# Decode attention: scores of the far old keys on VectorE, with key positions on partitions, and a far softmax of its own

## The chip, the cores and the metric

The kernel runs on one core of a Trainium2 chip. Its time is the device time of one execution in microseconds (us). TensorE (PE) multiplies matrices into PSUM, VectorE (DVE) and ScalarE (ACT) work elementwise and along rows, GpSimd (POOL) does small elementwise work, SyncE (SP) issues nearly all DMAs. Each engine runs its own instructions in the order of the program.

## What is computed

One decoder layer for 256 prompt tokens and 8 decode sequences of 8 new tokens (320 columns in all): a SwiGLU block, a token mixer, a second SwiGLU block. The mixer has an mLSTM branch and a branch of dilated attention with 8 heads of 128. The change is in the attention of the decode tokens. Cut to that:

```python
PATTERNS = ((128, 1), (512, 4), (2048, 16))          # window, dilation
for (w, d), bias in zip(PATTERNS, biases):
    idx = qi[:, None] - d * jnp.arange(w // d + 1)[None, :]
    s = jnp.einsum('bthe,btjhe->bhtj', q, k_all[:, idx]) + bias.T[None, :, None, :]
    m = jnp.max(s, axis=-1)
    p = jnp.exp(s - m[..., None])
    num, den = jnp.einsum('bhtj,btjhe->bthe', p, v_all[:, idx]), jnp.sum(p, axis=-1)
# the three (num, den, m) are joined by their maxima; 2048 old positions in the cache
```

Of the old positions the last 512 are near: all of them are multiplied, and a mask says how often each counts. The 96 far positions of a query (distance 528 to 2048 in steps of 16) are its own: query t of the 8 sees the positions 16 m + t, so the 8 queries of a sequence have 768 far positions between them and share none.

## The kernel before

All large weights are streamed: a chunk is 512 KB (four blocks of 128 rows by 256 columns). SP loads it (raw, 5 buffers), ScalarE casts it to hi, VectorE subtracts to get lo (3 buffers each, `split_upto`, L196 and L197), and TensorE runs 24 foreground matmuls (fg) with it. `run_job` (L242) goes through the chunks; with `split_upto(ci + HLB)` the chunk two ahead is split before chunk ci is multiplied. A chunk of casts can start when TensorE is done with the chunk whose buffer it takes.

All other work is written as Python generators that `run_job` steps between chunks: `every` at each chunk, `even` and `odd` at every second, `slow` at 8 of 15. `later(fn, n)` calls fn n chunks on; the DMAs are issued so. Background matmuls (bg, four PSUM tiles) stand in TensorE's program ahead of the chunk's own.

`sample_attention` (L586) is the only generator in `slow`. A unit u is a half of the heads (hg) and a sequence (b): 16 units, five steps each.
- Step 1: `pv(u - 1)` (probabilities times values), `scores(u)`, the scaled output (osb, L713), `soft(u)` (add of bias and mask, maximum, exponential).
- Step 2: `make_qbd(u + 1)` on GpSimd: the queries of the next unit, masked so that row 32 h + 8 i + t of the score tile is head h, group i of the keys, query t.
- Step 3: `probs(u)`: transposes of the probabilities, copies to SBUF, the sums. Steps 4 and 5 issue key loads only.

The old keys of a unit come in four tiles kd (a head each, 640 KB): four groups of 320 keys, 128 near ones and 192 far ones. The score tile thus has 128 rows (4 heads x 4 groups x 8 queries) and 328 columns: 128 near, 192 far (of which a row keeps every eighth, the mask drops the others), 8 new ones. Four matmuls in four column groups of TensorE (`tile_position`) make one step over 32 of the 128 rows of a head:

```python
for j in range(4):
    for h in range(4):
        mm(sp[32 * h:32 * h + 32, 0:320], qbd[:, 4 * h + j], KD[4 * u + h][:, j], j == 0, j == 3,
           tile_position=(0, 32 * h))
```

The values are multiplied in 11 steps of the same kind: 4 near, 6 far, 1 new. Every fourth unit `combine` (L735) transposes outputs and writes them to DRAM; after the last unit they are read back (ar) for the branch's projection w_pa.

## Time and profile before

| | |
|---|---|
| time, median of 3 | 2692.55 us (2691.93 to 2692.73) |
| the profiled execution | 2691.65 us |
| its span | 2689.9 us |
| mean granted TensorE clock | 0.998 |
| moved by DMA | 554.46 MB, 206 GB/s |

The profile is of one execution. "Busy" of PE is the time in which a matmul was under way; matmuls overlap, so the cost of a group is read from the starts. The chain that ended last goes back from the last instruction to what released it, step by step; an engine's share of it is what a change on this engine alone could move. A row of a group ends with its busy time, the mean ns of one, and the idle time of its engine ahead of it with what ended that. L numbers are lines of the kernel before.

### The profile page before, as it was taken

How to read it: one execution, taken by the hardware profiler on the slowest of the kernel's cores; microseconds unless marked ns; L12 is line 12 of the kernel's file. 1: busy time of each engine (PE TensorE's matmuls, PEld its weight loads, DVE VectorE, ACT ScalarE, POOL GpSimd, SP SyncE). 2: the span in 40 equal slices, each digit the busy share in tenths (PEclk: the TensorE clock that was granted, in tenths of full speed). 3: DMA queues.
4: the chain of work that ended last, by engine and by line, in shares of the span. 5: the costliest groups of instructions: out<-in, count | busy, mean ns of one | idle time of the engine just before them, and what ended most of it. 6: DMA issues, size and time to landing. Idle time of an engine off the chain costs nothing.

```text
span 2689.9 us, 49935 instructions
## 1 busy us (share of the span) xinstructions
PE 2674.8 (99%) x21176; PEld 2639.2 (98%) x21176; DVE 1430.7 (53%) x1706; ACT 1075.2 (40%) x1337; POOL 178.7 (7%) x222
## 2 busy tenths in 40 slices
PE   9999999999999999999999999999999999999998
PEld 9999999999999999999999999999999999999998
DVE  6544444444446554666655555655444454444445
ACT  5333333333335333455443444444333333333344
POOL 0100000000000000112211100000000000000000
PEclk9999999999999999999999999999999999999999
DMA  7554545445546678899999976655455454445443
GB/s 240 162 164 163 163 159 165 160 158 161 167 155 199 226 261 285 290 347 318 343 348 329 334 280 217 204 184 164 157 165 161 162 163 162 160 154 172 161 152 131
DMA packets 186684, 554.46 MB, mean 206 GB/s; under 512 B 26192, under 2 KB 53336, under 8 KB 186460
## 3 DMA queue, kind: packets, MB, share of 16 engines
q1 hardware_dynamic: 185740, 549.95, 60.5%
q8 instruction: 166, 2.72, 0.4%
q10 hardware_dynamic: 720, 1.31, 0.1%
q14 instruction: 58, 0.48, 0.1%
HBM read 519.98 MB, written 31.20 MB: 205 GB/s over the span
## 4 chain that ended last, share of the span: by engine, by line
PE 98%; DVE 1%; DMA 0%; ACT 0%; issue 0%; SPq 0%; DVEq 0%; ACTq 0%
PE fg L114 93%; PE bg L114 5%; PE bg L311 1%; DMA x<-in_x_t_dram 0%; DVE lo L197 0%; DVE x L1509 0%; DMA raw<-in_w_in_dram 0%; ACT hi L196 0%; DVE rows L781 0%; SPq L111 0%; ACT xh L1434 0%; DVE rows L790 0%; ACT lg L1497 0%; ACT hi L1424 0%; DVE x L1363 0%
## 5 line engine op out<-in xcount | busy, mean ns | idle before, releaser
L197 DVE TENSOR_TENSOR lo<-raw,hi 128x1024 fp32r<-128x1024 f32 (+1 forms) x780 | 958.1, 1235 | 919.4 <-ACT hi L196 895.9
L114 PE MATMUL fg<-xh,hi 128*128 128x320 f32 x4232 | 1271.4, 301 | 1.5 <-ACT hi L1424 1.5
L114 PE MATMUL fg<-xh,lo 128*128 128x320 f32 x4232 | 1261.6, 299 | 0.5 <-DVE lo L197 0.5
L114 PE MATMUL fg<-xl,hi 128*128 128x320 f32 x4232 | 1261.4, 299 | 0.0
L196 ACT CAST hi<-raw 128x1024 fp32r<-128x1024 f32 (+1 forms) x780 | 797.3, 1026 | 1039.6 <-PE fg L114 920.4
L114 PEld LDWEIGHTS fg<-xh,hi 128*128 128x128 f32 x4232 | 798.5, 189 | 8.9 <-issue 5.8
L114 PEld LDWEIGHTS fg<-xl,hi 128*128 128x128 f32 x4232 | 798.7, 189 | 0.8
L114 PEld LDWEIGHTS fg<-xh,lo 128*128 128x128 f32 x4232 | 798.6, 189 | 0.9 <-DVE lo L197 0.7
L114 PE MATMUL fg<-hh,hi 128*128 128x320 f32 x1408 | 421.3, 299 | 0.0
L114 PE MATMUL fg<-hl,hi 128*128 128x320 f32 x1408 | 421.0, 299 | 0.0
L114 PE MATMUL fg<-hh,lo 128*128 128x320 f32 x1408 | 421.0, 299 | 0.0
L114 PEld LDWEIGHTS fg<-hh,hi 128*128 128x128 f32 x1408 | 266.1, 189 | 0.1
L114 PEld LDWEIGHTS fg<-hl,hi 128*128 128x128 f32 x1408 | 266.1, 189 | 0.1
L114 PEld LDWEIGHTS fg<-hh,lo 128*128 128x128 f32 x1408 | 266.1, 189 | 0.0
L422 POOL TENSOR_TENSOR gt<-gt,rstd 128x640 f32<-128x640 f32 x44 | 68.2, 1549 | 1753.8 <-ACT gt L421 1753.8
L114 PE MATMUL fg<-bh,hi 128*128 128x320 f32 x512 | 153.3, 299 | 0.0
L114 PE MATMUL fg<-bl,hi 128*128 128x320 f32 x512 | 153.1, 299 | 0.0
L114 PE MATMUL fg<-bh,lo 128*128 128x320 f32 x512 | 153.1, 299 | 0.0
L114 PEld LDWEIGHTS fg<-bh,hi 128*128 128x128 f32 x512 | 96.8, 189 | 0.2 <-issue 0.2
L114 PEld LDWEIGHTS fg<-bl,hi 128*128 128x128 f32 x512 | 96.8, 189 | 0.0
L114 PEld LDWEIGHTS fg<-bh,lo 128*128 128x128 f32 x512 | 96.8, 189 | 0.0
L410 ACT CAST hh<-hf 128x640 fp32r<-128x640 f32 x44 | 34.7, 789 | 143.9 <-DVE hf L428 143.9
(266 smaller groups left out, 1217.6 us busy)
## 6 DMA issues: line engine op xcount, KB each, us to landing
raw<-in_w_in_dram SPq DMA_DIRECT2D x176, 512.0 KB
raw<-in_w_ffb_in_dram SPq DMA_DIRECT2D x176, 512.0 KB
raw<-in_w_ffa_in_dram SPq DMA_DIRECT2D x172, 512.0 KB
raw<-in_w_ffa_out_dram SPq DMA_DIRECT2D x80, 512.0 KB
kd<-in_old_k_dram SPq DMA_DIRECT2D x64, 640.0 KB
vt<-in_old_v_dram SPq DMA_DIRECT2D x80, 512.0 KB
raw<-in_w_ffb_out_dram SPq DMA_DIRECT2D x80, 512.0 KB
raw<-in_w_out_dram SPq DMA_DIRECT2D x32, 512.0 KB
```

The source lines that it names most:

```text
L114: T.matmul(out, a, b, start=start, stop=stop, **kw)
L196: S.copy(hi[:, :nk], t[:, :nk])
L197: V.tensor_tensor(lo[:, :nk], t[:, :nk], hi[:, :nk].bitcast(F32), op=OP.subtract)
L311: T.transpose(out, in_, ident[:k, :k])
L410: S.copy(h, xe)
L422: G.tensor_tensor(gt, gt, bcast(rstd, 2), op=OP.mult)
```

## The change

The keys are laid out anew on the host: near_k holds the near keys of two heads in a tile (nk, 512 KB, 32 of them), far_k the far keys with positions on partitions (fk, 128 positions x 2 groups x 512 columns of four heads, 512 KB, three a unit). Partition 16 t + i holds a position of query t. The score tile has 138 columns: 128 near, 8 new, one for the far maximum and one for the far sum.

- `aq_evac` transposes the decode queries to rows (two transposes for each pair of heads) and writes them to DRAM (qt_d). `load_qr` reads the 8 query rows of a unit back, each to 16 partitions (qr, 256 KB).
- `far_dots(u, n)`: VectorE multiplies a far tile by qr; the sums over the 128 columns of a head are a reduction on VectorE (n = 0 and 2) or eight activations with a sum on ScalarE (n = 1).
- `far_max`, `far_sum`: bias, the maximum over the 96 positions of a query by two 32x32 transposes, the exponential, the sum along the row. Four matmuls (fr by tsel) add the maximum and the sum over partitions and put them into columns 136 and 137 of the score tile.
- `soft` takes its maximum over near, new and far maximum; `probs` works out the two factors rw. `far_probs` spreads the far probabilities to the columns of their queries (pf), so that they need no transpose. `pv` makes near and far outputs apart, and VectorE adds the second to the first with its factor.
- The far work of unit u + 1 stands in the steps of unit u: dots 0 in step 1, dots 1 in step 2, dots 2 and the maximum in step 4, the sum in step 5. The loop over the units begins two steps later.
- In `numer` of the mLSTM an Abs on ScalarE takes the place of two VectorE instructions.

```diff
-SCOLS = 328
+SCOLS = 138
...
-            mk[:, i, t, 128 + t:320:8] = 0.0
             if i == 0:
-                mk[:, i, t, 320:328] = _logmult(t - np.arange(8))
+                mk[:, i, t, 128:136] = _logmult(t - np.arange(8))
+                mk[:, i, t, 136] = 0.0
+            mk[:, i, t, 137] = 0.0
...
+    tsel = (p[:, None] // 16 == q[None] % 8).astype(np.float32)
+    lead = (p[:, None] % 16 == 0).astype(np.float32)
+    c["mix"] = np.concatenate([bd, sel, sels, in4, qmask, cm, tsel, lead], axis=1)
...
-    RAWB, HLB, KDB = 5, 3, 6
+    RAWB, HLB, NKB, FKB = 5, 3, 3, 4
...
+        yield
+        yield
+        a = bg_tile()
+        for m in range(2):
+            tr(a[0:NS, m * 128:(m + 1) * 128], q[:, m, SEQ:NT])
+        s = m2_tile("qt")
+        S.copy(s[0:NS, 0:256], a[0:NS, 0:256])
+        later(lambda: dma(qt_d[:, p * 256:(p + 1) * 256], s[0:NS, 0:256]))
+        M["aq"] = p
...
+        def load_near(n):
+            if n < 32:
+                NK[n] = mxt([128, 2, 4, 128], "nk4", NKB, "nk")
+                dma(NK[n], I["near_k"][n].rearrange("p (h j c) -> p h j c", h=2, j=4))
+
+        def load_far(n):
+            if n < 48:
+                FK[n] = mxt([128, 2, 512], "fk", FKB, "fk")
+                dma(FK[n], I["far_k"][n].rearrange("p (a c) -> p a c", a=2))
+
+        def load_qr(u):
+            if u < 16:
+                hg, b = divmod(u, 8)
+                assert M["aq"] >= 2 * hg + 1
+                QR[u] = mxt([128, 512], "qr", 2, "qr")
+                dma(QR[u], raw_ap(qt_d[:], 8 * b * 1024 + hg * 512, [[1024, 8], [0, 16], [1, 512]]))
...
+        def far_dots(u, n):
+            if u > 15:
+                return
+            if n == 0:
+                SF[u] = mxt([128, 6, 4], "fs", 2, "fs")
+            t, sf = FK.pop(3 * u + n), SF[u]
+            V.tensor_tensor(t, t, bcast(QR[u], 2), op=OP.mult)
+            if n == 1:
+                for a in range(2):
+                    for h in range(4):
+                        x = t[:, a, h * 128:(h + 1) * 128]
+                        S.activation(x, x, AF.Copy, accum_out=sf[:, 2 + a, h:h + 1])
+            else:
+                V.tensor_reduce(sf[:, 2 * n:2 * n + 2].rearrange("p a h -> p (a h)"),
+                                t.rearrange("p a (h d) -> p (a h) d", h=4), op=OP.add, axis=AX.X)
+            later(lambda: load_far(3 * u + n + FKB), 1)
+
+        def far_max(u):
+            if u > 15:
+                return
+            sf = SF[u]
+            V.tensor_tensor(sf, sf, M["fb"][:, u // 8], op=OP.add)
+            V.tensor_reduce(fm[:, 0, 0:4], sf.rearrange("p c h -> p h c"), op=OP.max, axis=AX.X)
+            V.transpose(fm[:, 1], fm[:, 0])
+            V.tensor_reduce(fm[:, 2, 0:2], fm[:, 1].rearrange("p (s k) -> p s k", s=2), op=OP.max, axis=AX.X)
+            V.tensor_copy(fm[:, 1].rearrange("p (s k) -> p s k", s=2), bcast(fm[:, 2, 0:2], 16, 2))
+            V.transpose(fm[:, 2], fm[:, 1])
+            V.tensor_tensor(sf, sf, bcast(fm[:, 2, 0:4], 6), op=OP.subtract)
+            S.activation(sf, sf, AF.Exp)
+
+        def far_sum(u):
+            if u > 15:
+                return
+            V.tensor_scalar(fr[:, :, 0], fm[:, 2, 0:4], lead, None, op0=OP.mult)
+            V.tensor_reduce(fr[:, :, 1], SF[u].rearrange("p c h -> p h c"), op=OP.add, axis=AX.X)
+
+        def far_probs(u):
+            V.tensor_tensor(pf[:, 0:192].rearrange("p (a t) -> p a t", t=8),
+                            bcast(SF.pop(u).rearrange("p c h -> p (c h)"), 8, 2), bcast(tsel[:, 0:8], 24), op=OP.mult)
...
-        for _ in range(3):
-            yield
+        load_qr(0)
+        yield
+        load_qr(1)
+        yield
...
-                    mm(sp[32 * h:32 * h + 32, 0:320], qbd[:, 4 * h + j], KD[4 * u + h][:, j], j == 0, j == 3,
+                    mm(sp[32 * h:32 * h + 32, 0:128], qbd[:, 4 * h + j], NK[2 * u + h // 2][:, h % 2, j], j == 0, j == 3,
                        tile_position=(0, 32 * h))
             for h in range(4):
                 c = (4 * hg + h) * 64 + 8 * b
-                mm(sp[32 * h:32 * h + 32, 320:328], M["qS"][:, c:c + 32], M["kS"][:, c:c + 8],
+                mm(sp[32 * h:32 * h + 32, 128:136], M["qS"][:, c:c + 32], M["kS"][:, c:c + 8],
                    tile_position=(0, 32 * h))
+            for h in range(4):
+                mm(sp[32 * h:32 * h + 32, 136:138], tsel, fr[:, h], tile_position=(0, 32 * h))
...
-            V.tensor_reduce(sm[:, 0, 0:1], s, op=OP.max, axis=AX.X)
+            V.tensor_reduce(sm[:, 0, 0:1], s[:, 0:137], op=OP.max, axis=AX.X)
...
-            S.activation(s, s, AF.Exp, bias=sm[:, 3, 0:1], accum_out=sm[:, 4, 0:1])
+            S.activation(s[:, 0:136], s[:, 0:136], AF.Exp, bias=sm[:, 3, 0:1], accum_out=sm[:, 4, 0:1])
+            S.activation(s[:, 136:137], s[:, 136:137], AF.Exp, bias=sm[:, 3, 0:1])
...
-            cs = [(128, 0, 8 * i, i // 2, i % 2) for i in range(4)]
-            cs += [(128, 1, 8 * i, 2 + i // 2, i % 2) for i in range(4)]
-            cs += [(128, 2, 16 * i, 4, i) for i in range(2)]
-            cs += [(128, 3, 0, 5, None)]
-            for n, (k, slot, c, pc, half) in enumerate(cs):
-                v = VT[u, pc] if half is None else VT[u, pc][:, half]
+            cs = [(0, 8 * i, VT[u, i // 2][:, i % 2]) for i in range(4)] + [(1, 0, VT[u, 5])]
+            for n, (slot, c, v) in enumerate(cs):
                 for h in range(4):
-                    mm(ob[32 * h:32 * h + 32, 0:128], pts[0:k, slot, 32 * h + c:32 * h + c + 32],
-                       v[0:k, h * 128:(h + 1) * 128], n == 0, n == len(cs) - 1, tile_position=(0, 32 * h))
+                    mm(ob[32 * h:32 * h + 32, 0:128], pts[:, slot, 32 * h + c:32 * h + c + 32],
+                       v[:, h * 128:(h + 1) * 128], n == 0, n == 4, tile_position=(0, 32 * h))
+            for c in range(6):
+                v = VT[u, 2 + c // 2][:, c % 2]
+                for h in range(4):
+                    a = 8 * (4 * c + h)
+                    mm(ob[32 * h:32 * h + 32, 128:256], pf[:, a:a + 32],
+                       v[:, h * 128:(h + 1) * 128], c == 0, c == 5, tile_position=(0, 32 * h))
...
-            tr(pt[:, 128:256], s[:, 128:256])
-            tr(pt[0:72, 256:384], s[:, 256:328])
-            S.copy(pts[:, 0:2, 0:128], pt[:, 0:256].rearrange("p (c n) -> p c n", c=2))
-            V.tensor_copy(pts[0:64, 2, 0:128], pt[0:64, 256:384])
-            S.copy(pts[64:128, 2, 0:120], pt[0:64, 264:384])
-            V.tensor_copy(pts[0:8, 3, 0:128], pt[64:72, 256:384])
+            tr(pt[0:8, 128:256], s[:, 128:136])
+            S.copy(pts[:, 0, 0:128], pt[:, 0:128])
+            S.copy(pts[0:8, 1, 0:128], pt[0:8, 128:256])
             V.transpose(sm[:, 1], sm[:, 4])
             V.tensor_reduce(sm[:, 5, 0:8], sm[:, 1].rearrange("p (i t) -> p t i", i=4), op=OP.add, axis=AX.X)
-            V.reciprocal(sm[:, 5, 0:8], sm[:, 5, 0:8])
             V.transpose(sm[:, 6], sm[:, 5])
-
+            V.scalar_tensor_tensor(rw[:, 0:1], s[:, 137:138], s[:, 136:137], sm[:, 6, 0:1], op0=OP.mult, op1=OP.add)
+            V.reciprocal(rw[:, 0:1], rw[:, 0:1])
+            V.tensor_tensor(rw[:, 1:2], rw[:, 0:1], s[:, 136:137], op=OP.mult)
+        far_dots(0, 0)
+        yield
+        far_dots(0, 1)
         qbd = make_qbd(0)
+        yield
+        far_dots(0, 2)
+        far_max(0)
+        yield
+        far_sum(0)
...
+            far_dots(u + 1, 0)
...
-                S.activation(o4[:, (u - 1) % 4], ob[:, 0:128], AF.Copy, scale=sm[:, 6, 0:1])
+                o = o4[:, (u - 1) % 4]
+                S.activation(o, ob[:, 0:128], AF.Copy, scale=rw[:, 0:1])
+                V.scalar_tensor_tensor(o, ob[:, 128:256], rw[:, 1:2], o, op0=OP.mult, op1=OP.add)
...
             values(u, 4, 0, 2)
-            keys(u, 0)
-            yield
+            later(lambda u=u: load_near(2 * u + NKB), 1)
+            later(lambda u=u: load_qr(u + 2), 2)
+            yield
+            far_probs(u)
+            far_dots(u + 1, 1)
             if u < 15:
                 qbd = make_qbd(u + 1)
-            keys(u, 1)
+            later(lambda u=u: load_near(2 * u + 1 + NKB), 1)
             values(u, 1, 3, 5)
             yield
             probs(s)
-            keys(u, 2)
             if u == 6:
                 q4 = make_q4(1)
             yield
-            keys(u, 3)
-            yield
+            far_dots(u + 1, 2)
+            far_max(u + 1)
+            yield
+            far_sum(u + 1)
...
-            V.tensor_scalar(rd, B[:, 0:NT], -1.0, None, op0=OP.mult)
-            V.tensor_tensor(rd, rd, B[:, 0:NT], op=OP.max)
+            S.activation(rd, B[:, 0:NT], AF.Abs)
```

TensorE, the start of a unit (pts and pf are probabilities, vt and vn values; kd, nk, kS keys; qbd, qS queries). Before:

```order
L114 MATMUL bg<-vt,pts 32x128 x40
L114 MATMUL bg<-vn,pts 32x128 x4
L114 MATMUL bg<-kd,qbd 32x320 x16
L114 MATMUL bg<-kS,qS 32x8 x4
L114 MATMUL fg<-xh,hi 128x320
```

The same place after the change:

```order
L117 MATMUL bg<-vt,pts 32x128 x16
L117 MATMUL bg<-vn,pts 32x128 x4
L117 MATMUL bg<-vt,pf 32x128 x24
L117 MATMUL bg<-nk,qbd 32x128 x16
L117 MATMUL bg<-kS,qS 32x8 x4
L117 MATMUL bg<-fr,mixc 32x2 x4
L117 MATMUL fg<-xh,hi 128x320
```

The value products stay 44, in two groups; the scores have 128 columns in place of 320; four matmuls of two columns follow.

VectorE in step 1 of a unit, between two chunks' lo. Before:

```order
L197 TENSOR_TENSOR lo<-raw,hi 128x1024
L660 TENSOR_TENSOR ss<-bg,ttab 128x328
L661 TENSOR_REDUCE sm<-ss 128x1
L662 STREAM_TRANSPOSE sm<-sm 128x32
```

After:

```order
L200 TENSOR_TENSOR lo<-raw,hi 128x1024
L664 TENSOR_TENSOR fk<-fk,qr 128x1024
L671 TENSOR_REDUCE fs<-fk 128x8
L801 SCALAR_TENSOR_TENSOR osb<-bg,rw,osb 128x128
L738 TENSOR_TENSOR ss<-bg,ttab 128x138
L739 TENSOR_REDUCE sm<-ss 128x1
L740 STREAM_TRANSPOSE sm<-sm 128x32
```

Three instructions have come ahead of the add that reads the scores (bg) from PSUM.

VectorE in step 4 after the change, where before only loads were issued (fk far keys, fs far scores, fm far maxima):

```order
L200 TENSOR_TENSOR lo<-raw,hi 128x1024
L664 TENSOR_TENSOR fk<-fk,qr 128x1024
L671 TENSOR_REDUCE fs<-fk 128x8
L679 TENSOR_TENSOR fs<-fs,fb 128x24
L680 TENSOR_REDUCE fm<-fs 128x4
L681 STREAM_TRANSPOSE fm<-fm 128x32
L682 TENSOR_REDUCE fm<-fm 128x2
L683 COPY fm<-fm 128x32
L684 STREAM_TRANSPOSE fm<-fm 128x32
L685 TENSOR_TENSOR fs<-fs,fm 128x24
L200 TENSOR_TENSOR lo<-raw,hi 128x1024
```

Nine instructions stand between the lo of one chunk and the lo of the next.

More of the change, by code (lines that the diff above doesn't have):

```diff
@@ L321, in decoder_kernel @@
     vs_d = dp.tile([NS, 1024], F32, name="vs_d")
+    qt_d = dp.tile([NS, 1024], F32, name="qt_d")
     qs_d = [dp.tile([128, 256], F32, name=f"qs_d{i}") for i in range(2)]
@@ L625, in make_q4 @@
             return q4
-        for n in range(KDB):
-            load_k(n)
+        def far_dots(u, n):
[34 more added lines that the diff above has]
+                            bcast(SF.pop(u).rearrange("p c h -> p (c h)"), 8, 2), bcast(tsel[:, 0:8], 24), op=OP.mult)
+        for n in range(NKB):
+            load_near(n)
+            yield
+        for n in range(FKB):
+            load_far(n)
             yield
@@ L1222, in mixer_open @@
         M["tanh"] = True
-        M["qk"], M["ak"], M["av"], M["mo"] = 0, -1, -1, -1
+        M["fb"] = c([128, 2, 6, 4], "fb")
+        dma(M["fb"], I["bias_f"].rearrange("p (g c h) -> p g c h", g=2, c=6))
+        M["qk"], M["aq"], M["ak"], M["av"], M["mo"] = 0, -1, -1, -1, -1
         spawn(sample_attention(), slow)
@@ L1539, in _lay_out @@
     g, c = np.arange(4)[:, None], np.arange(128)[None]
-    k, r = (v.reshape(1, -1) for v in np.meshgrid(np.arange(24), np.arange(8), indexing="ij"))
-    pos = np.concatenate([1536 + 128 * g + c, 16 * (24 * g + k) + r], axis=1)
-    old = a.pop("cache_k")[0][:, pos].reshape(NB, 4, 320, 2, 4, 4, 32)
-    a["old_k"] = old.transpose(3, 0, 4, 1, 6, 5, 2).reshape(64, 128, 1280)
+    ck = a.pop("cache_k")[0]
+    near = ck[:, 1536 + 128 * g + c].reshape(NB, 4, 128, 2, 2, 2, 4, 32)
+    a["near_k"] = near.transpose(3, 0, 4, 1, 7, 5, 6, 2).reshape(32, 128, 1024)
+    m = 16 * np.arange(6)[:, None] + np.arange(16)[None]
+    far = (16 * m[:, None] + np.arange(8)[None, :, None]).reshape(6, 128)
+    fk = ck[:, far].reshape(NB, 3, 2, 128, 2, 512)
+    a["far_k"] = fk.transpose(4, 0, 1, 3, 2, 5).reshape(48, 128, 1024)
     cv = a.pop("cache_v")[0].reshape(NB, PAST, 2, 512)
-    far = (16 * np.arange(96)[:, None] + np.arange(8)).reshape(4, 192)
-    vpos = np.concatenate([1536 + np.arange(512), far[:, 0:128].reshape(512), far[:, 128:].reshape(256)])
+    vpos = np.concatenate([1536 + np.arange(512), far.reshape(768)])
     a["old_v"] = cv[:, vpos].reshape(NB, 5, 2, 128, 2, 512).transpose(4, 0, 1, 3, 2, 5).reshape(16, 5, 128, 1024)
@@ L1559, in _lay_out @@
         np.broadcast_to(512 + t[None] - 128 * g[..., None] - c[:, None], (4, 8, 128)),
-        np.broadcast_to(2048 - 16 * (24 * g[..., None] + k[:, None]), (4, 8, 192)),
         np.broadcast_to(t - np.arange(8)[None], (4, 8, 8))], axis=2)
-    bs = rel[_bucket(np.maximum(dist, 0))].reshape(4, 8, SCOLS, 2, 4)
+    bs = np.zeros((4, 8, SCOLS, 2, 4), np.float32)
+    bs[:, :, 0:136] = rel[_bucket(np.maximum(dist, 0))].reshape(4, 8, 136, 2, 4)
+    bf = rel[_bucket(2048 - 16 * m)].reshape(6, 16, 2, 4).transpose(1, 2, 0, 3).reshape(16, 48)
+    a["bias_f"] = np.tile(bf, (8, 1))
     a["bias_s"] = bs.transpose(4, 0, 1, 3, 2).reshape(128, 2 * SCOLS)
```

28 lines of the change are left out of this document (14 added, 14 removed).

## The prediction

> **What bounds the kernel now.** I read the busy shares first, then the chain that ended last, then the stretches of the mixer stage.
>
> ```profile
> PE 2674.8 (99%) x21176; PEld 2639.2 (98%) x21176; DVE 1430.7 (53%) x1706; ACT 1075.2 (40%) x1337; POOL 178.7 (7%) x222
> ...
> PE 98%; DVE 1%; DMA 0%; ACT 0%; issue 0%; SPq 0%; DVEq 0%; ACTq 0%
> ```
>
> TensorE is 98% of the chain that ended last. So a microsecond taken off TensorE's program is a microsecond off the time, as long as TensorE is not made to wait instead. The change touches the decode attention, 16 units, one for each half of the heads and each sequence. Where they lie, and how full the stretches are (columns: us, then busy time of each engine, granted clock, DMA share, GB/s):
>
> ```profile
> L713 ACT ACTIVATE osb<-bg,sm x16: 357/368/368, 1013.5 to 1612.6; 128x128 f32<-128x128 f32 x16
> ...
> 1150.00:1200.00 50.00, 50.00 (x465) 47.28 (x463) 36.31 (x75) 27.12 (x45) 11.61 (x20) 1.00 0.92 334
> ...
> 1250.00:1300.00 50.00, 50.00 (x555) 46.04 (x552) 33.15 (x64) 25.35 (x42) 9.79 (x14) 1.00 0.98 366
> ...
> 1400.00:1450.00 50.00, 50.00 (x471) 46.98 (x470) 26.14 (x35) 19.94 (x29) 9.94 (x17) 1.00 0.98 358
> ```
>
> The scaled output of a unit (osb) is made 16 times between 1013.5 and 1612.6 us, so a unit takes 599.1 / 15 = 39.9 us. In these stretches TensorE is busy for 50.00 of 50 us at clock 1.00. VectorE has 14 to 24 us of 50 left, the DMA engines a few per cent. So the question has two halves: what TensorE loses, and whether VectorE can take what it is given without making TensorE late.
>
> **TensorE, term by term.** The second unit shows every kind of matmul in question, back to back:
>
> ```profile
> 1010.80 2.39 PE L114 MATMUL bg<-vt,pts 128*32 128x128 f32 x80
> 1013.01 0.40 PE L114 MATMUL bg<-vn,pts 128*32 128x128 f32 x8
> 1013.23 2.34 PE L114 MATMUL bg<-kd,qbd 128*32 128x320 f32 x32
> 1015.38 0.22 PE L114 MATMUL bg<-kS,qS 128*32 128x8 f32 x8
> 1015.53 0.87 PE L311 MATMUL bg<-ident,v 128*128 128x128 f32 x6
> ...
> 988.98 0.33 PE bg L311 x3
> ```
>
> The starts tell the cost, since ends overlap (the last row is a piece of the chain: three transposes). Each program matmul in fp32 is two records. The scores with 320 keys go from 1013.23 to 1015.38: 2.15 us for 32 records, 67 ns each. The 88 records of probabilities times values have the form 128*32 by 128x128 and go from 1010.80 to 1013.23: 2.43 us, 27.6 ns each.
>
> - Scores. The keys per group fall from 320 to 128, with the same 16 program matmuls. Their form becomes exactly that of the value products (32 stationary columns, 128 moving ones, four column groups in turn), so I price them by that row: 32 x 27.6 ns = 0.88 us. Saved: 2.15 - 0.88 = 1.27 us a unit, **20.3 us** in 16.
> - Values. 11 steps of four before, 5 near and 6 far steps of four after, same form: 0.
> - Transposes of the probabilities. Three before (0.33 us, last row), two after: 0.11 us a unit, **1.8 us**.
> - New: four matmuls of two columns (fr) that carry the far maximum and sum into the score tile. Nearest row: the eight records with 8 columns, 1015.38 to 1015.53, 0.15 us. Added **2.4 us**; from both sides 0 and 16 x 0.22 = 3.5 us.
> - New: two transposes for each of four query pairs, at a place of their own. At 0.11 us each **0.9 us**; up to twice that if entering and leaving the foreground costs as much again.
>
> Sum: 20.3 + 1.8 - 2.4 - 0.9 = **18.8 us** less TensorE work, from 16.8 to 21.2 with the two unknowns at their ends. The Abs in place of two VectorE instructions happens in four heads and touches no TensorE row; I count it as nothing.
>
> **What VectorE and ScalarE get for it.** Durations by form (mean ns after the comma), one evacuation of the foreground (sg), two tiny instructions in a row, and a ScalarE activation with the read of its sum along the row:
>
> ```profile
> L197 DVE TENSOR_TENSOR lo<-raw,hi 128x1024 fp32r<-128x1024 f32 x748 | 936.2, 1258 | 912.8 <-ACT hi L196 889.3 <-DMA vt<-in_old_v_dram 4.7 <-PE bg L311 2.0
> L660 DVE TENSOR_TENSOR ss<-bg,ttab 128x328 f32<-128x328 f32 x16 | 8.0, 499 | 34.3 <-PE bg L114 34.2
> L661 DVE TENSOR_REDUCE sm<-ss 128x1 f32<-128x328 f32 x16 | 7.9, 495 | 0.6
> L694 DVE COPY pts<-bg 64x128 f32<-64x128 f32 x16 | 4.4, 277 | 4.1 <-ACT pts L693 4.0
> L662 DVE STREAM_TRANSPOSE sm<-sm 128x32 f32<-128x32 f32 x16 | 3.4, 212 | 0.5
> L541 DVE TENSOR_REDUCE ns<-s 128x1 f32<-128x128 f32 x8 | 2.2, 274 | 0.0
> L385 DVE TENSOR_TENSOR sg<-fg,rstd 128x640 f32<-128x640 f32 x20 | 16.5, 824 | 16.5 <-PE fg L114 16.4
> ...
> 975.94 0.21 DVE L663 TENSOR_REDUCE sm<-sm 128x8 f32<-128x32 f32 x1
> 976.18 0.18 DVE L664 TENSOR_SCALAR sm<-sm 128x32 f32<-128x32 f32 x1
> ...
> 937.54 0.40 ACT L544 ACTIVATE s<-s,ns 128x128 f32<-128x128 f32 x1 [2.55 <-DVE ns L543]
> 937.85 0.18 ACT L544 ACTIVATION_READ_ACCUMULATOR s<-s,ns 128x1 f32 x1
> 937.94 0.49 ACT L545 ACTIVATE s<-s,ns 128x256 f32<-128x256 f32 x1
> ```
>
> For each unit VectorE gets three products of 1024 columns (1.26 us, as lo: 3.8), two reductions of 1024 inputs (274 ns at 128 and 495 at 328 give 1.1 ns an input, so 1.26 us: 2.5), nine tiny instructions of the far softmax (0.21 us, as the transpose: 1.9), the spread of 192 probabilities (0.35) and a second scaling of the output (0.28, as the copy of 128 columns). It gives back 0.4 us of the shorter add and maximum (328 columns to 138) and some 0.2 us of copies. That is 8.2 us a unit, 131 us in all. One of the three products is summed by ScalarE, eight activations at 0.40 us (937.54 to 937.94): 3.2 us, with two small exponentials about 3.6.
>
> In a stretch of 50 us (1.25 units) that is 10.3 us of VectorE and 4.5 of ScalarE. The fullest one, 1150 to 1200, goes to 46.6 and 31.6 of 50. Both still fit, so on average TensorE stays the bound. What counts is the order inside a chunk of weights, since lo and hi of the next chunks stand in the same queues behind the new work.
>
> ```profile
> 1196.78 2.36 DVE L197 TENSOR_TENSOR lo<-raw,hi 128x1024 fp32r<-128x1024 f32 x2 [1.74 <-ACT hi L196]
> ...
> 1200.13 0.30 PE L114 MATMUL fg<-xh,hi 128*128 128x320 f32 x1
> ...
> 1200.20 1.04 ACT L196 CAST hi<-raw 128x1024 fp32r<-128x1024 f32 x1 [1.46 <-PE fg L114]
> ...
> ACT hi L196 <- PE fg L114: 920.4, 450, 2.9
> ...
> DVE ss L660 <- PE bg L114: 34.2, 14, 3.7
> ...
> 1186.02 3.26 PE fg L114 x24
> ```
>
> The cast of chunk c+2 waits until TensorE is done with chunk c-1 (three buffers; the wait sums to 920.4 us). At 1200.13 TensorE begins a chunk, and 0.07 us later that cast starts. Cast 1.04 and lo 1.23 end 2.3 us after the chunk's start; TensorE wants them two chunks of 3.26 us after it, at 6.5. That is 4.2 us of slack without background matmuls; the tightest place that I found has 2.1 (the first lo of the pair ends near 1198.0, its chunk starts at 1200.13).
>
> - First step of a unit (product, reduction, output scaling: 2.8 us). It stands ahead of the add that waits for TensorE's scores, a wait of 34.2 us in 14 now. It fills that wait, and TensorE has 3.6 us of background there. Cover: good. Without it, 2.8 against the 4.2 us of slack.
> - Second step (spread, product, then ScalarE's eight sums). VectorE ends lo at 2.3, the product at 3.9; ScalarE is done at 7.1, the next cast at 8.2, its lo at 9.4. TensorE wants that at 9.8: 0.4 us to spare.
> - Fourth step (product, reduction, seven tiny instructions in a row, an exponential that ScalarE waits for): 2.3 + 1.26 + 1.26 + 7 x 0.24 (975.94 to 976.18) = 6.5, exponential to 6.8, cast 7.9, lo 9.1: 0.7 us to spare. An evacuation of 0.82 us in the same chunk uses that up.
>
> Background matmuls of other work in the same chunk lengthen the slack, evacuations shorten it. So a stall is a few tenths in a few of 32 places; I take **1 us**, with 0 and 11 us (0.35 us in all 32) as ends.
>
> Other moves. TensorE's two-column matmuls wait for the far sum, which VectorE gets a step earlier, some 7 us ahead. On SP the key loads move as many bytes as before (64 x 640 KB against 80 x 512 KB); 16 loads of queries copied to 16 partitions each (256 KB) and four small writes are new: 4.2 MB, 11.5 us at the 366 GB/s of the fullest stretch, spread over 600 us.
>
> ```profile
> kd<-in_old_k_dram SPq DMA_DIRECT2D x64, 640.0 KB
> ...
> SPq L111 <- DVE lo L197: 1906.6, 701, 7.7
> ...
> L410 ACT CAST bh<-ar x4: 807/810/812, 1656.4 to 1658.5; 128x640 fp32r<-128x640 f32 x4
> ```
>
> A far load waits on SP for its buffer, and raw loads stand behind it; but SP waits for a later lo of VectorE at that place anyway (1906.6 us), so nothing is lost. The unit loop starts two of its steps later, 3.75 chunks or about 14 us; the last output moves from 1612.6 to about 1626, and its reader casts at 1656.4. Covered; if that cover were gone, at most those 14 us would show.
>
> **Against the profiled execution** (2691.65 us, span 2689.9): 2691.65 - 18.8 + 1.0 = 2673.9. The median of the runs shown, 2692.55, lies 0.9 above it, so I predict **2674.8** for the median.
>
> **Rivals.**
>
> 1. Late chunks in both steps of every unit: 0.35 us at 32 places, 11 us, **2685**. For it: the spare 0.4 and 0.7 us are small, and 1150 to 1400 holds much other VectorE work. Against it: background matmuls stand in most of these chunks. 15%.
> 2. The scores don't shrink with their columns, since weight loading sets their pace: then 20.3 us is not there, and 2692.55 - 1.8 + 2.4 + 0.9 + 1 = **2695**; with half of it, 2685. Against it: the value products have the same weights at 27.6 ns. 3%, of which most is the half.
> 3. The queries' loads hit the fullest stretches and weights come late: at most 11.5 us, **2686**. Against it: 0.02 to 0.12 of the DMA time is free. 2%.
> 4. Slower: VectorE's products are held up by GpSimd and VectorE becomes the bound.
>
> ```profile
> L883 DVE SCALAR_TENSOR_TENSOR pre<-pre,y x8: 784/818/1280, 1109.7 to 1331.1; 128x640 f32<-128x640 f32 x8
> ...
> L639 POOL TENSOR_TENSOR qbd<-q,mixc x16: 1263/1270/1855, 967.3 to 1541.7; 128x512 f32<-128x512 f32 x16
> ```
>
> An instruction with two inputs in SBUF took 818 ns mostly and 1280 at worst, and GpSimd's qbd 1270 and 1855: they do disturb each other here. In the second step qbd stands right beside a product. If each of the three products is held for a whole qbd, VectorE gets 3.8 us more a unit; the fullest stretch comes to 51.4 of 50, and the second and fourth steps are late by 0.9 and 0.6 us: 24 us in 16 units, and some 6 us for the full stretches. That gives 2674.8 + 29 = **2704**. It decides from 1.5 us of stall a unit (24 / 16). Against it: GpSimd is busy for only 8 to 12 of 50 us, and one product of three has qbd beside it. 5%. [...]
>
> **Numbers.** Forecast case 75%, from 2671 (nothing stalls, the two-column matmuls free) to 2678. The range takes in rivals 1 to 3: 2671 to 2686.5. A measurement can tell about 0.2% (5.4 us) from no change: faster from 2687.2 down. Faster 0.91 (forecast, rival 1, rival 3, part of 2), same 0.04, slower 0.05.
>
> **What would show it.** Scores at some 28 ns a record and a set of 0.9 us right: the first term. Fewer than 0.3 us for the fr matmuls: the fourth. TensorE idle for lo or hi between 1000 and 1630 us would show the stalls, by their sum; VectorE over 47 of 50 us in 1150 to 1200, and products well above 1.26 us, would show rival 4; raw loads named as releasers rival 3. I am wrong if the scores stay above 50 ns a record, or if TensorE waits more than 13 us in sum.

## The result, and the profile after

| | before | after |
|---|---|---|
| time, median (lowest to highest) | 2692.64 us (2691.93 to 2692.93) | 2711.01 us (2708.07 to 2711.96) |
| ratio, 95% interval | 1 | 1.0067 (1.0049 to 1.0084) |
| profiled execution / its span | 2691.65 / 2689.9 us | 2710.33 / 2708.4 us |
| mean granted TensorE clock | 0.998 | 0.995 |

The changed kernel is 18 us **slower**; 18 us faster was forecast. The page of the changed kernel, its busy times and the shares of its chain:

```profile
PE 2670.2 (99%) x21296; PEld 2645.6 (98%) x21296; DVE 1545.3 (57%) x1954; ACT 1107.7 (41%) x1633; POOL 188.3 (7%) x224
...
PE 50%; DVE 1%; DMA 1%; ACT 0%; issue 0%; SPq 0%; POOL 0%; DVEq 0%; POOLq 0%
```

The busy shares hardly moved, and PE still has 99%. The shares of the chain now add up to 53%: followed back from the end, it reaches only to 1271 us and breaks off there. So the 50% of TensorE, where it had 98%, doesn't measure the loss; it points at the place, the mixer stage, where the chain leaves TensorE again and again. A part of it there, in order of time (start, us, what):

```profile
1298.53 1.15 DVE fk L664
1299.70 0.73 ACT fk L669 x5
...
1302.15 0.93 ACT hi L199
...
1303.45 0.41 PE bg L314 x2
```

A far product on VectorE holds ScalarE's sums, they hold a cast and the copies behind it, and these hold TensorE. The stretches of the mixer stage in the changed kernel (columns as before):

```profile
1150.00:1200.00 50.00, 50.00 (x503) 48.31 (x494) 41.51 (x92) 26.96 (x64) 8.18 (x17) 1.00 0.94 335
...
1250.00:1300.00 50.00, 45.24 (x416) 43.41 (x416) 40.52 (x77) 23.45 (x44) 12.89 (x20) 0.93 0.80 273
1300.00:1350.00 50.00, 45.51 (x438) 42.90 (x437) 38.63 (x74) 28.82 (x74) 11.63 (x20) 0.97 0.92 324
...
1400.00:1450.00 50.00, 50.00 (x506) 48.02 (x508) 38.46 (x69) 23.17 (x51) 11.73 (x14) 1.00 0.98 349
...
1000.00:1500.00 500.00, 477.17 (x4752) 459.48 (x4753) 380.31 (x722) 239.84 (x567) 87.54 (x138) 0.98 0.92 320
```

TensorE is idle for 500 - 477.17 = 22.8 us between 1000 and 1500, where before it was idle for none; and from 1250 to 1350 its clock is 0.93 and 0.97, where it was 1.00. VectorE, the engine that got the work, is at 38 to 42 of 50 us in these rows. So no engine is full, and TensorE waits all the same.

Who waits for what, in the changed kernel (us in total, times, longest):

```profile
ACT hi L199 <- PE fg L117: 794.4, 381, 4.2
...
ACT fs L686 <- DVE fs L685: 87.5, 16, 7.7
...
ACT fk L669 <- DVE fk L664: 47.7, 16, 5.1
...
PE fg L117 <- ACT hi L199: 6.5, 4, 3.5
PE fg L117 <- DVE lo L200: 5.8, 8, 1.2
PE bg L117 <- POOL ks L1060: 4.0, 2, 3.2
```

Two waits are new, both of ScalarE for VectorE, once in every unit: the far exponential (fs, step 4) for the maximum, 5.5 us each time, and the eight sums (fk, step 2) for the product, 3.0 us. The healthy wait, that of the cast for TensorE to give back a buffer, fell from 920.4 us in 450 to 794.4 in 381: at some 70 chunks the cast no longer arrives early. The last three rows are TensorE's own waits, over the whole span. Before, it waited 0.5 us for a lo and for none of the mixer's hi or ks. Only about half of the new idle stands ahead of weights (hi and lo); the rest stands ahead of background matmuls that wait for ks, pts (2.3 us), ptS (2.2 us) or C (1.3 us), each made from results of ScalarE or VectorE. The timeline of the changed kernel at the longest of these waits, one engine after the other:

```profile
1260.38 1.03 ACT L199 CAST hi<-raw 128x1024 fp32r<-128x1024 f32 x1
...
1261.95 0.81 ACT L1111 ACTIVATE kw<-bg,aeT 128x256 f32<-128x256 f32 x2
1270.48 0.22 ACT L686 ACTIVATE fs<-fs 128x24 f32<-128x24 f32 x1 [7.72 <-DVE fs L685]
1270.61 0.92 ACT L967 ACTIVATE y<-pre,gv 128x256 f32<-128x256 f32 x2
1271.43 1.03 ACT L199 CAST hi<-raw 128x1024 fp32r<-128x1024 f32 x1
...
1260.81 2.47 DVE L969 SCALAR_TENSOR_TENSOR y<-pre,gv,y 128x256 f32<-128x256 f32 x6
1263.20 1.21 DVE L200 TENSOR_TENSOR lo<-raw,hi 128x1024 fp32r<-128x1024 f32 x1
1264.34 0.61 DVE L1106 TENSOR_TENSOR z<-z,bg 128x448 f32<-128x448 f32 x1
1264.96 1.38 DVE L1108 TENSOR_TENSOR vs<-vq,vs 32x512 fp32r<-32x512 f32 x2
1266.38 1.23 DVE L664 TENSOR_TENSOR fk<-fk,qr 128x1024 f32<-128x1024 f32 x1
1267.63 1.22 DVE L671 TENSOR_REDUCE fs<-fk 128x8 f32<-128x1024 f32 x1
...
1270.27 0.18 DVE L685 TENSOR_TENSOR fs<-fs,fm 128x24 f32<-128x24 f32 x1
...
1272.52 0.40 PE L117 MATMUL fg<-xh,hi 128*128 128x320 f32 x1 [3.53 <-ACT hi L199]
```

VectorE works without a pause from 1260.81 on: the mLSTM's convolution, a lo, two more mLSTM groups, then the far product, reduction and maximum. ScalarE reaches the far exponential at 1262.76 (1261.95 + 0.81) and stands there for 7.72 us. The cast of the next chunk is queued behind it, starts at 1271.43 and ends at 1272.46; TensorE, dry since 1268.99, starts at 1272.52. Nothing overtook the waiting exponential: in this trace VectorE's 1954 instructions and ScalarE's 1461 (its 1633 less 160 reads of a sum and 12 table loads) start in the order of the program.

What comes behind such a wait, in the same kernel (stretches; the column behind the busy times is the granted clock):

```profile
1268.99:1272.52 3.53, 0.00 (x1) 0.01 (x1) 2.54 (x12) 1.98 (x4) 0.00 (x0) 1.00 0.86 234
1273.10:1279.90 6.80, 5.61 (x21) 5.62 (x22) 4.12 (x6) 5.58 (x8) 2.28 (x3) 0.50 0.92 325
1280.00:1284.00 4.00, 4.00 (x74) 3.50 (x77) 3.23 (x10) 3.66 (x7) 0.04 (x1) 1.00 0.63 208
```

After 3.53 us of idle TensorE gets half its clock for 6.8 us: the foreground matmuls from 1274.71 to 1279.51 start 0.267 us apart, those from 1258.64 to 1264.89 started 0.136 us apart. It is busy for 5.61 us of the 6.8, so this costs 5.61 / 2 = 2.8 us more. The records of the clock have four such pieces between 1000 and 1500 us in the changed kernel: 3.4 us from 1211.7, 6.8 from 1273.1, 3.4 from 1303.9 and 3.4 from 1392.6, in sum 17.0 us. Less the 1.2 us of idle within them, 15.8 us ran at half the clock, so 7.9 us were lost.

### The profile page after: what moved, and what is told of

Its sections match the earlier page's. It is cut to its first block, busy times and chain, and to the rows that moved or that the text cites. A ratio compares the mean times of both kernels' runs of the same rounds, so it can differ in the third digit from the quotient of the medians.

```text
span 2708.4 us, 50803 instructions
## 1 busy us (share of the span) xinstructions
PE 2670.2 (99%) x21296; PEld 2645.6 (98%) x21296; DVE 1545.3 (57%) x1954; ACT 1107.7 (41%) x1633; POOL 188.3 (7%) x224
## 3 DMA queue, kind: packets, MB, share of 16 engines
q10 hardware_dynamic: 720, 1.31, 0.1%
## 4 chain that ended last, share of the span: by engine, by line
PE 50%; DVE 1%; DMA 1%; ACT 0%; issue 0%; SPq 0%; POOL 0%; DVEq 0%; POOLq 0%
PE fg L117 48%; PE bg L117 2%; DMA vt<-in_old_v_dram 0%; DVE lo L200 0%; DMA q<-qk_d 0%; ACT fk L669 0%; PE bg L314 0%; DVE fk L664 0%; DVE x L1602 0%; ACT hi L199 0%; DVE vs L1108 0%; SPq L114 0%; DVE y L969 0%; DVE C L1166 0%; POOL re L1200 0%
## 5 line engine op out<-in xcount | busy, mean ns | idle before, releaser
L199 ACT CAST hi<-raw 128x1024 fp32r<-128x1024 f32 (+1 forms) x780 | 795.1, 1026 | 903.9 <-PE fg L117 794.4
```

Source lines behind the costliest of these rows:

```text
L199: S.copy(hi[:, :nk], t[:, :nk])
```

## The experiments

Theory ("order"): the new ScalarE instructions wait for VectorE and stand ahead of casts; TensorE runs dry and then gets half its clock. Rivals: VectorE has too much work in all ("load"); loads come late; the saving on TensorE isn't there. All medians stand beside runs of the kernel before on the same chip (2692.64 us for the changed kernel, 2691.66 to 2691.89 for the others), so a difference between the changed kernel and an experiment is uncertain by about 1 us. Idle is 500 us less PE's busy time in 1000 to 1500 us; half clock is the time of such pieces there; VectorE's busy time is that of the whole span.

| kernel | median us | ratio to before (95%) | idle us | half clock us | VectorE us |
|---|---|---|---|---|---|
| after | 2711.01 | 1.0067 (1.0049, 1.0084) | 22.8 | 17.0 | 1545.3 |
| e1 no far math | 2675.74 | 0.9942 (0.9927, 0.9956) | 1.3 | 0 | 1423.1 |
| e2 exponential late | 2700.24 | 1.0031 (1.0020, 1.0043) | 16.8 | 13.6 | 1546.7 |
| e3 sums late | 2688.90 | 0.9989 (0.9980, 0.9999) | 9.0 | 10.2 | 1546.6 |
| e4 both late | 2683.58 | 0.9969 (0.9958, 0.9981) | 8.0 | 3.4 | 1548.7 |
| e5 both late, third earlier | 2686.18 | 0.9978 (0.9969, 0.9987) | 8.7 | 10.2 | 1546.2 |
| e6 sums on VectorE, exponential late | 2683.45 | 0.9966 (0.9953, 0.9978) | 5.1 | 6.8 | 1564.2 |
| e7 two query loads | 2709.28 | 1.0062 (1.0048, 1.0076) | 20.3 | 20.4 | 1546.1 |
| e8 ScalarE blocks in before | 2699.42 | 1.0028 (1.0017, 1.0038) | 4.7 | 6.8 | 1429.4 |
| e9 four cast buffers | 2708.08 | 1.0058 (1.0044, 1.0072) | 20.5 | 17.0 | 1548.2 |
| e10 spread | 2692.10 | 0.9999 (0.9991, 1.0008) | 11.3 | 17.0 | 1563.5 |
| e11 product, then sums, in before | 2703.53 | 1.0042 (1.0028, 1.0056) | 6.1 | 0 | 1455.6 |
| e12 product beside sums, in before | 2691.97 | 1.0001 (0.9991, 1.0010) | 0.0 | 0 | 1456.6 |

### e1: is TensorE's saving there?

```diff
+G.memset(fr, 0.0)
 def far_dots(u, n):
-    V.tensor_tensor(t, t, bcast(QR[u], 2), op=OP.mult)
...
+    FK.pop(3 * u + n)
     later(lambda: load_far(3 * u + n + FKB), 1)
 def far_max(u):
-    V.tensor_tensor(sf, sf, M["fb"][:, u // 8], op=OP.add)
...
+    pass
```

far_sum and far_probs are empty in the same way; TensorE's matmuls and all loads are those of the changed kernel.

> Left out: the far products, their sums, the far maximum, exponential, sum and spread (VectorE and ScalarE); TensorE's matmuls and all loads, the queries' too, stay as in the changed kernel. Theory (order in ScalarE's and VectorE's queues makes TensorE wait; TensorE's saving is real): the prediction's sum without any stall, 2691.65 - 18.8 = 2673 us, in a range of 2670 to 2676, and TensorE idle under 2 us between 900 and 1650 us. Rival (TensorE's saving is not there, or the new loads make weights late): 2690 or more.

2675.74 us. One stretch of this kernel:

```profile
1000.00:1500.00 500.00, 498.74 (x5125) 485.55 (x5124) 306.51 (x572) 228.24 (x388) 88.34 (x148) 1.00 0.96 345
```

TensorE idles for 1.3 us and keeps its clock. So the saving on TensorE is there, the loads alone do no harm, and the 35 us between this kernel and the changed one come with the far instructions on VectorE and ScalarE. It leaves open whether by their amount or their order, and whether loads come late when VectorE holds their buffers longer (here it reads no far tile).

### e2, e3, e4: the two waits moved, the work kept

e2 moves the far exponential from the end of far_max (step 4) to the beginning of far_sum (step 5):

```diff
 def far_max(u):
...
-    S.activation(sf, sf, AF.Exp)
 def far_sum(u):
+    S.activation(SF[u], SF[u], AF.Exp)
```

e3 moves the eight sums from far_dots(u + 1, 1) in step 2, where they become far_sums, to step 3, behind the near probabilities; e4 does both:

```diff
             probs(s)
+            far_sums(u + 1)
```

> One edit to the changed kernel: the far exponential of ScalarE moves from step 4, where it waits for nine VectorE instructions, to the start of step 5. Theory (ScalarE stands still in front of that wait, with the casts of weights behind it): the waits of the far exponential, 87.5 us in 16, nearly vanish, the stalls behind it too, about half of the gap: 2690 to 2700 us. Rival (VectorE's total work is the bound, whatever the order): no change, 2707 to 2714 us.

> One edit to the changed kernel: ScalarE's eight sums move from step 2, right behind the product that they wait for, to step 3. Theory: their waits, 47.7 us in 16, vanish, and with them the stalls at 1125, 1211 and 1303 us and the half clock that follows: 2692 to 2702 us. Rival (total work of VectorE, or of ScalarE): no change, 2707 to 2714 us.

> Both moves together. Theory: nearly all stalls go, the granted clock stays at 1.00, 2674 to 2684 us. Rival (total work): still over 2700 us. If the two hide each other: nearer to the better one of the two alone.

e2 took 10.8 us off, a little less than its range; e3 took 22.1 off, better than its range; e4, with both, 27.4. All three have every instruction of the changed kernel. The waits of e4:

```profile
ACT hi L199 <- PE fg L117: 862.7, 419, 2.9
...
ACT fs L700 <- DVE fs L695: 7.0, 5, 2.2
...
ACT fk L682 <- DVE fk L664: 2.3, 1, 2.3
```

135.2 us of ScalarE waiting became 9.3, and the casts are early again at 419 chunks. VectorE's busy time is 3 us more than in the changed kernel. That speaks against the load, and the order's range held for e4, at its upper end; that the clock would stay at 1.00 did not hold (one piece of 3.4 us). The sum of a wait is no price, though: the exponential alone (e3, still 84.2 us of waits for it) costs 2688.90 - 2683.58 = 5.3 us, the sums alone (e2, 48.0 us of waits) 2700.24 - 2683.58 = 16.7 us.

### e5: step 4 relieved

```diff
             far_sums(u + 1)
+            far_dots(u + 1, 2)
...
-            far_dots(u + 1, 2)
             far_max(u + 1)
```

> Both moves of the run before (far exponential at the start of step 5, ScalarE's eight sums behind the near probabilities of step 3), and besides VectorE's third product and reduction moved from step 4 to the end of step 3, so that step 4 holds only the seven small instructions of the maximum. Order theory (what counts is how long VectorE's and ScalarE's queues are at one time): the stall of 3.97 us at 1260, where lo stood behind spread, product, reduction and the small ones, shrinks or goes, and with it its half clock: 2677 to 2683 us. Load theory (VectorE's total work sets it): as before, 2682 to 2686 us, since no work is taken away.

2686.18, no better than e4. The stall of 3.97 us at lo became one of 1.46, and another of 3.40 us came up at the mLSTM's ks at 1335. The expectation of the order theory missed; the place of a burst moved, not its cost.

### e6: more work for VectorE, fewer waits

```diff
-            if n == 1:
-                for a in range(2):
...
-            else:
-                V.tensor_reduce(sf[:, 2 * n:2 * n + 2].rearrange("p a h -> p (a h)"),
+            V.tensor_reduce(sf[:, 2 * n:2 * n + 2].rearrange("p a h -> p (a h)"),
```

So all three thirds are summed by VectorE; the exponential is late as in e2.

> The second third's sums as one VectorE reduction (1.22 us) in place of ScalarE's eight (2.35 us), and the far exponential at the start of step 5. VectorE gets 16 times 1.22 = 19.5 us more work than in any kernel so far, ScalarE has no sums to wait for. Load theory: slower than the run with the late exponential alone, 2702 to 2715 us. Order theory: no ScalarE instruction waits for the far work in front of a cast, so faster than it, 2682 to 2696 us, with what is left in the places where lo stands behind a burst on VectorE.

The busy times on the page of e6:

```profile
PE 2660.1 (99%) x21296; PEld 2641.1 (99%) x21296; DVE 1564.2 (58%) x1970; ACT 1073.9 (40%) x1377; POOL 191.5 (7%) x224
```

VectorE has 18.9 us more than in the changed kernel (17.5 more than e2), and ScalarE 35.8 us less than in e2. Its fullest stretch in e6:

```profile
1200.00:1250.00 50.00, 50.00 (x489) 48.98 (x489) 46.42 (x86) 24.61 (x44) 11.95 (x24) 1.00 1.01 367
```

VectorE is at 46.42 of 50 us there, with TensorE busy for 50.00 beside it; the time is 2683.45, 27.6 us under the changed kernel and 16.8 under e2. The load theory gave 2702 to 2715. It falls. ScalarE's smaller work isn't the cause either: e4 keeps it all and has the same time. With e4 this is the fastest version that computes the whole, 0.3% below the kernel before.

### e7: the loads

```diff
-            if u < 16:
+            if 1 < u < 16:
+                QR[u] = QR[u % 2]
+            elif u < 16:
```

> The changed kernel with queries loaded for two units only and used again for the others, so 14 loads of 256 KB fewer (the outputs of 14 units are those of other queries). Order theory: the same places stall, 2706 to 2712 us. Load theory of the transfers (late chunks or late queries cost the time): 2 to 11 us faster, 2698 to 2707 us.

2709.28 (2707.08 to 2710.70): within the scatter of the changed kernel, at most a microsecond or two faster. The traces say the same of the other loads: in the changed kernel no stall of TensorE over 0.3 us between 1000 and 1500 us is put down to a load, and no wait of a cast is put down to a load of the mixer's weights; e1 has 11.5 us of such waits, without harm. Late loads aren't the cause.

### e8: ScalarE blocked in the kernel before

```diff
             s = soft(u, sp)
+            for _ in range({3: 6, 6: 12, 9: 18, 12: 24}.get(u, 0)):
+                S.activation(scr[:, 0:128], scr[:, 0:128], AF.Copy, accum_out=scr[:, 128:129])
```

> The kernel before, with 6, 12, 18 and 24 sums on a scratch tile put into ScalarE's queue behind the near exponential of units 3, 6, 9 and 12 (about 1.8, 3.5, 5.3 and 7.0 us by 0.29 us each; nothing waits for their results and they wait for nothing of VectorE's). Order theory: TensorE runs dry for the length of the block less one to two microseconds that the casts are ahead: near 0, 2, 3.5 and 5 us, and after the gaps of about 2 us and more the clock is at half for 3.4 or 6.8 us, 1.7 or 3.4 us each: in sum 12 to 20 us, 2704 to 2712 us. If the half clock belongs to something else of the change (more VectorE work, other matmuls), it doesn't come here: 8 to 11 us, 2700 to 2704 us. If TensorE's lead covers more than that: 2693 to 2698 us.

2699.42, between the ranges. The sums came 0.43 us apart, not 0.29, so the blocks were 2.6, 5.2, 7.7 and 10.3 us. The stretches around the third and around the fourth:

```profile
1300.00:1350.00 50.00, 50.00 (x470) 47.45 (x469) 30.58 (x59) 32.65 (x76) 13.16 (x26) 1.00 0.88 302
1350.00:1400.00 50.00, 49.83 (x456) 47.14 (x455) 33.37 (x58) 22.34 (x36) 7.78 (x9) 1.00 0.96 354
...
1471.96:1476.48 4.52, 0.02 (x1) 0.02 (x1) 2.01 (x3) 4.43 (x13) 1.34 (x2) 0.73 0.00 0
1476.48:1480.80 4.32, 4.32 (x14) 3.93 (x15) 4.28 (x5) 2.18 (x4) 3.59 (x3) 0.50 0.70 247
```

The block of 7.7 us (1338.5 to 1346.2) cost TensorE 0.2 us; the one of 10.3 (1463.1 to 1473.4) cost 4.52 us idle and 6.8 us at half clock. The clock fell 2.1 us into the gap, so TensorE worked at half the clock for the 4.32 us of the last row only, which costs 2.2. 2691.7 + 4.7 + 2.2 = 2698.6, where the profiled execution took 2699.04: the whole cost but half a microsecond. Two things follow. The half clock belongs to a gap, not to the change. And a block on ScalarE alone is far cheaper than I had put it: at these places TensorE has some 6 to 7.5 us in hand (10.3 - 4.5 and 7.7 - 0.2). In the changed kernel a wait of the same 7.7 us cost 3.53 plus the clock; there VectorE, which makes the lo and the mLSTM's links, was itself behind for as long. That this makes the difference is read from the rows, not tried.

### e9: one more cast buffer

```diff
-    RAWB, HLB, NKB, FKB = 5, 3, 3, 4
+    RAWB, HLB, NKB, FKB = 4, 4, 3, 3
```

> The changed kernel in its own order, with four buffers for the two parts of a weight chunk in place of three (paid for by one raw buffer and one buffer of far thirds), so that hi and lo of a chunk can be made one chunk, about 6 us, earlier. Order theory: lo of a chunk comes 6 us earlier against its use, so the stalls at hi and lo (1125, 1272, 1391) go, with their half clock; those behind ks, pts and C, which do not come from chunks, stay: 2688 to 2700 us. If ScalarE or VectorE as a whole were short of time, more buffers would fill up and run empty again: 2704 to 2712 us.

2708.08: the order theory's range missed. The stalls at hi and lo did go, but for one of 0.72 us, and others took their place. The same spot on e9's timeline:

```profile
1271.12 0.22 ACT L686 ACTIVATE fs<-fs 128x24 f32<-128x24 f32 x1 [7.72 <-DVE fs L685]
...
1278.62 0.53 ACT L1211 ACTIVATE re<-bg,epst 128x320 f32<-128x320 f32 x1
...
1279.20 1.08 PE L117 MATMUL bg<-vt,pts 128*32 128x128 f32 x16 [4.16 <-ACT re L1211]
```

ScalarE waits for the same 7.72 us. Now the weights are there, but the mLSTM's re, behind that wait in the same queue, is late, and TensorE stands 4.16 us ahead of the values, a background matmul in its program. So "the cast of the next chunk is late" was too narrow: in this run whatever TensorE needs next from ScalarE is late, and a deeper buffer for one of them only changed which. The run isn't clean, though: for the raw buffer that it gave up, casts waited for raw loads, 12.6 us in four waits, of which the changed kernel has none. One of 6.37 us ends at 1147.9, 3 us ahead of a new stall of 3.12. What the fourth buffer alone is worth stays open.

### e10: VectorE's bursts spread

```diff
-            far_dots(u + 1, 0)
+            if u == 0:
+                far_dots(1, 0)
...
             probs(s)
+            far_dots(u + 1, 2)
...
-            far_dots(u + 1, 2)
...
             far_sum(u + 1)
+            far_dots(u + 2, 0)
```

Beside this it is e6.

> The run with all sums on VectorE and the late exponential, and its bursts spread: the first third's product and reduction moved from step 1 (beside the near softmax) to the end of step 5 of the unit before, the third third's from step 4 (beside the maximum) to the end of step 3. VectorE's steps are then about 2.2, 2.9, 3.6, 1.4 and 2.6 us in place of 4.7, 2.9, 1.2, 3.8 and 0.2. Order theory: the remaining stalls of 1.93 us (lo, 1257) and 1.84 us (C, 1324) and their half clock shrink: 2676 to 2681 us. Load theory: no less work, 2681 to 2685 us.

2692.10, 8.7 us worse than e6 with the same work: both theories missed. TensorE stalled for 2.48 us at 1127, 3.40 at 1270 and 3.42 at 1340 in place of 1.93 and 1.84. VectorE's timeline ahead of the middle one:

```profile
1264.06 1.22 DVE L664 TENSOR_TENSOR fk<-fk,qr 128x1024 f32<-128x1024 f32 x1
1265.32 1.22 DVE L665 TENSOR_REDUCE fs<-fk 128x8 f32<-128x1024 f32 x1
1266.45 0.82 DVE L971 SCALAR_TENSOR_TENSOR pre<-pre,y 128x640 f32<-128x640 f32 x1
```

The product and the reduction that moved to step 5 stand ahead of the mLSTM's pre. ScalarE waited 3.38 us for that pre, with two casts and kr behind it, and TensorE for kr. So an even load per step didn't help. What decided at this place is which instruction of other work, that ScalarE waits for, stands behind the burst.

### e11 and e12: the wait alone

In step 2 of each unit of the kernel before, with scratch tiles va and sb (e11; in e12 x is cut from sb):

```diff
+            for _ in range(3):
+                V.tensor_tensor(va, va, va, op=OP.mult)
+            for i in range(8):
+                x = va[:, 128 * (i % 2):128 * (i % 2) + 128]
+                S.activation(x, x, AF.Copy, accum_out=sb[:, 256:257])
             if u < 15:
                 qbd = make_qbd(u + 1)
```

> The kernel before, with three products of 384 on a scratch tile put into VectorE's queue in step 2 of each unit (about 1.5 us in all) and eight sums over that tile's columns behind them in ScalarE's (2.3 us): ScalarE waits for VectorE there, as in the changed kernel. Order theory: 2695 to 2706 us, with ScalarE waits of some 5 us in front of casts. If it is work and not waiting that costs, this run and the next have the same time.

> The same products and the same eight sums as in the run before, but the sums are over another scratch tile, so ScalarE waits for none of VectorE's products. Order theory: 2692 to 2694 us, as the kernel before. Load theory: as the run before, to 1 us.

The new row among the waits of e11:

```profile
ACT va L729 <- DVE va L727: 48.8, 16, 5.3
```

ScalarE waits 48.8 / 16 = 3.05 us in each unit, as in the changed kernel (some 5 were expected); the eight sums then take 3.5 us in e11 and e12, where 2.3 were expected. The stretch of e11:

```profile
1000.00:1500.00 500.00, 493.91 (x4746) 465.84 (x4744) 317.65 (x583) 254.93 (x549) 86.75 (x140) 1.00 0.89 318
```

And of e12:

```profile
1000.00:1500.00 500.00, 500.00 (x4904) 473.51 (x4906) 322.93 (x586) 259.47 (x554) 88.24 (x144) 1.00 0.90 324
```

Same instructions, same busy times (VectorE 1455.6 and 1456.6 us, ScalarE 1123.9 and 1124.2). Where the sums read the product, the time is 2703.53. Where they read another tile, ScalarE has no such wait, and it is 2691.97, as the kernel before. **The dependency costs 11.6 us, the work nothing**, in a kernel that has nothing else of the change. Half the clock had no part here.

The idle in the records is 6.1 us of these 11.6. Set against the starts of the same weight matmuls in e12, twelve jumps make 10.2 us (1.0 of the difference is there at 960 us already, ahead of the first added instruction); the largest is 1.92 where the records show 1.31 idle. The idle is counted from the modelled end of the last matmul, so each stall is some tenths longer than it reads. The changed kernel against e1, whose TensorE programs are the same, falls back by 36.1 us over such starts; 35.9 is the difference of the two profiled executions (2710.33 and 2674.46). So all of the loss lies in TensorE's waits and its slower clock in this stage.

## Why the prediction was wrong

The forecast was 2674.8 us, the median is 2711.01. Point by point:

**TensorE's terms were right.** The rows of one unit in the changed kernel:

```profile
1027.31 1.06 PE L117 MATMUL bg<-nk,qbd 128*32 128x128 f32 x32
1028.18 0.23 PE L117 MATMUL bg<-kS,qS 128*32 128x8 f32 x8
1028.24 0.22 PE L117 MATMUL bg<-fr,mixc 128*32 128x2 f32 x8
1028.39 0.40 PE L117 MATMUL fg<-xh,hi 128*128 128x320 f32 x1
```

The scores take 1028.18 - 1027.31 = 0.87 us (0.88 predicted), 27 ns a record; the two-column matmuls 0.15 (0.15 predicted). In sum, e1's execution less its idle, 2674.46 - 1.3 = 2673.2, is 18.5 us under the 2691.65 of before: 18.8 was predicted. Rival 2 is out.

**VectorE's and ScalarE's work was a little over-sized**: 1545.3 - 1430.7 = 115 us of VectorE against 131 predicted, 33 of ScalarE against 58 (in part since the sums come 0.29 us apart, not 0.40). "Both still fit, so on average TensorE stays the bound" held too, to 46.42 of 50 us in e6.

**The step that failed is the next one**: "0.4 us to spare" in the second step, "0.7 us to spare" in the fourth, hence "a stall is a few tenths in a few of 32 places; I take 1 us, with 0 and 11 us as ends". That sum let the far work begin on VectorE as soon as the lo of its chunk was done, at 2.3 us after the chunk's start. In the rows of 1260 to 1272 the product begins 2.0 us behind that lo (1266.38 against 1264.41), with 2.0 us of mLSTM work between them and 2.4 us of convolution ahead of the lo; I had named a single evacuation of 0.82 as what could stand there. What I called a spare was that of an empty queue. The far exponential and the sums then hold ScalarE for 5.5 and 3.0 us a unit, and everything behind them: casts, the mLSTM's kr (e10), kf and re (e9), and the attention's pts, each of which feeds TensorE. I had listed only hi and lo as queued behind, and that failed by itself too. At 1205 the product did begin right behind its lo (1205.08, the lo ended at 1204.90), as in my sum for the second step. But the sums held ScalarE until 1208.68, a cast stood behind them, and only then ks and kf, which GpSimd joins to the ks of a background matmul: TensorE stood for 3.19 us until 1211.62. By e2 to e4 the wait in the second step cost more (16.7 us) than the one in the fourth (5.3). In all the cost was 21.5 us more idle than in e1 (22.8 - 1.3) by the records, 7.9 us of the clock, and the 6.7 us that are left of 36.1, some tenths for each stall, which the records' modelled ends hide.

**The clock was not in the sum at all.** I priced a stall by its length. Each stall of 2.3 us and more between 1200 and 1400 was followed by half the clock for 3.4 or 6.8 us, so the stall of 3.53 us cost 2.8 us beside its length.

**Rival 1** (late chunks in both steps, 11 us) had the right place and a third of the size: it took a stall to be the same few tenths everywhere. The stalls are few and long: eleven of over 0.8 us, ten of them between 1125 and 1392 us, where the mLSTM's work shares the queues. **Rival 4** forecast the sign by another mechanism, products held up by GpSimd. The products' durations in the changed kernel (least, median, most):

```profile
L664 DVE TENSOR_TENSOR fk<-fk,qr x48: 1208/1218/2295, 963.7 to 1597.2; 128x1024 f32<-128x1024 f32 x48
```

The median is 1218 ns, against 1260 priced; 2295 was the worst. Each of the six over 1300 ns (1341 to 2295) ran beside an instruction of GpSimd. But all 48 together took 61.9 us, 3.4 more than 48 medians, where this rival counted 3.8 in each unit, so medians and e6 leave no room for that mechanism as the cause. **Rival 3** was at most a microsecond or two (e7). My own bound for being wrong, TensorE waiting for more than 13 us in sum, was passed at 22.8.

**What stays open.** Which of the places stalls, and how long, wasn't predicted by any rule that I tried: e5, e9 and e10 missed. e4 and e6 keep 8 us over e1, at places where lo, ks or C stands behind a VectorE burst; no order that removes them was found.

## What to carry to other kernels

Where an instruction is added to an engine's queue, ask first whether it waits for another engine, and then what stands in *that* engine's queue ahead of what it waits for; the price is the delay of everything behind it that feeds the bound engine, not its own length (11.6 us against 0.1 for the same work). Put the waiting instruction a step later, or do its work on the engine that it waits for, even when that engine is the busier one (e6 against e2: 17.5 us more VectorE work and 16.8 us less time). And price a stall of TensorE with the clock that it loses afterwards (7.9 us of the changed kernel's time).
